# A streaming encoder layer on one core: token operands of the pairs in a pool of their own, two branch jobs run together, convolutions spread differently

## The chip, the cores and the metric

The kernel runs on one core of one Trainium2 chip. Its time is device microseconds (us) of one execution. Three executions of the kernel before took 2276.99, 2281.00 and 2281.24 us, median 2281.0. The profiled execution is another one, of 2278.88 us.

The core's engines run side by side, each in the order of its own queue: TensorE (PE, matmuls), VectorE (DVE), ScalarE (ACT), GpSimd (POOL) and SyncE (SP), which here issues all the DMAs.

## The reference

One inference step of a layer with 1024 channels, for 1024 prompt tokens and 32 sample tokens. All is float32:

```
x    = layer_norm(x)
proj = x @ w_in                                   # 1024 x 17424
y_a  = a * conv3(..) * silu(z_a)                  # branch 0
y_b  = RGLRU(conv4(x_b)) * silu(z_b)              # branch 1
y_c  = silu(LN(conv31(GLU(..)))) * silu(z_c)      # branch 2
y_d  = RMSNorm(gated_delta(silu(conv4(q,k,v)))) * silu(z_d)   # branch 3
mixed = sum over n of sigmoid(gate_n) * (y_n @ w_branch[n])
x    = layer_norm(ALPHA * x + mixed @ w_out)
```

The convolutions are causal and depthwise, with 3, 4, 31 and 4 taps. The new convolution and recurrence states are outputs too.

## The kernel before, in words

Activations lie channels by tokens: a tile is 128 channels x 1056 tokens (1024 + 32), 528 KB. A float32 product is made of three matmuls on rounded halves: the high part of the weights by the high and by the low part of the activations, and the low part of the weights by the high part (wh by xh, wh by xl, wl by xh). The code that splits a weight is `wsplit`: one DMA (L177), one ACT cast (wh, L179), one DVE subtraction (wl, L181).

The work goes in stages.

1. **Jobs.** A `Job` is one 128-channel output of an input projection: three chunks of 352 tokens, 24 matmuls each (L212), and per chunk an eviction by ACT or DVE. While they run, queues of generators are stepped between groups of eight matmuls (`bg`): the gated-delta work, the triangular elimination of branch D on DVE (`eliminate`, L546 and L547), short convolutions, and in `qc` the 31-tap convolutions of branch C (`c_conv`, one DVE step per tap, L297). The rate of a queue is the number of its steps per three calls of `bg`. The first four of the eight 31-tap convolutions (`N_CONV`) are made here; the input of the other four is written to DRAM (`d_cp`) for later.
2. **Pairs.** 36 `Pair`s compute two 128-channel outputs each by a seven-product scheme on quarters of the activations (L1046). Their token operands are built once (`build_t`): xh and xl themselves, and six tiles TH and TL for sums and differences (product operands t1, t2, t4). A product is 2 chunks of 12 matmuls. Each pair uses the three pairs of PSUM banks a, c and b once. Products 1, 3, 5 and 6 are added up in banks a: after products 1, 3 and 5, ACT copies the running sum away (`keep`, `mu`, L1058) before the next product adds to it, and after product 6 ACT evicts it (L1080). A queue `qm` steps in the pairs: the four late 31-tap convolutions, their statistics, then eight `b_mix` (branch B: convolution, gates with 18 matmuls L1153, a scan L1173).
3. **Branches**, in the order 0, 3, 2, 1. For each, eight staged tiles (`stage_y`: two loads `d_t` and `d_z`, one DVE multiply, L1274; branch 2 has more) are split into yh (ACT cast, L1247) and yl (DVE subtraction, L1248) by `put_y`, and eight branch jobs of 72 matmuls multiply them with `w_branch`, are scaled by a gate tile loaded from DRAM, and are added up in DRAM (`d_mix`). The first and the last job of a branch have their row tiles k as the outer loop over three banks (`all_chunks`, L224), the others take a chunk at a time (L212). The tiles for the next branch are staged while the jobs run.
4. **Output projection**, 9 token tiles (L1333), layer norm and store.

Memory is reused between stages: what the pairs use, xh, xl, TH and TL, lies on one stack (`xstack`), which is closed after the last pair; the tiles yh, yl and the sixteen staging tiles `st` are allocated in its place (`yp`). So the first load of branch 0 stands after the last product of the last pair. The instructions of an engine are put in their final order by a scheduler that also moves work forward; the order on each engine is therefore quoted from the built program where it matters.

Of the kernel before, what the change touches and what calls it, by code (L numbers as in the profile page):

```python
# [53 lines left out]
def encoder_step(ctx: ExitStack, tc: tile.TileContext, I, O):  # L54
# [173 lines left out]
    XR = (lambda k: xh[:, k, :], lambda k: xl[:, k, :])  # L228

# [589 lines left out]
    qc = queue("conv", 1.45)  # L819
    ORDER = "A0 A1 X0 C0 X1 A2 C1 X2 A3 C2 X3 A4 C3 X4 A5 C4 X5 C5 C6 C7"  # L820
    N_CONV = 4
# [122 lines left out]
    TH = {j: w2.tile([128, 4, HT], F32R, name=f"th{j}") for j in (1, 2, 4)}  # L944
    TL = {j: w2.tile([128, 4, HT], F32R, name=f"tl{j}") for j in (1, 2, 4)}
# [46 lines left out]
    class Pair:  # L992
# [10 lines left out]
        def prep(self):  # L1003
# [17 lines left out]
            split("21", a12, wpool, "wl")  # L1021
            yield
            dve.tensor_sub(a12, a12, s)
            dve.tensor_sub(a21, a11, a21)
            split("t3", a21, w2, "o3")
            yield
            split("t4", a22, w2, "o4")
            yield
            split("22", a12, w2, "o2")

        def run(self, step):
# [22 lines left out]
            def keep(name):  # L1054
                def then(c, b):
                    if c == 0:
                        mu[name] = w2.tile([128, HT], F32, name="mu", bufs=2)
                    act.copy(mu[name][:, c * HC:(c + 1) * HC], b)  # L1058
                return then
# [27 lines left out]
            product(4, "21", "b", True, plus(0, 0, "m1"), True)  # L1087
            product(5, "t3", "a", False, m7)
            product(6, "t4", "a", False, m4, True)
            product(7, "22", "c", False, plus(0, 1, "u1"), True)  # L1090

    def run_pairs(pairs, after):
# [4 lines left out]
        for n, p in enumerate(pairs):  # L1097
# [10 lines left out]
            def step(j):  # L1108
# [9 lines left out]
                elif j >= 6 and after is not None and nxt is None:  # L1118
                    after.load()
# [80 lines left out]
    qm = queue("mix", 0.52 * PARTS)  # L1200
# [37 lines left out]
    run_pairs(pairs, wb[branches[0]][0])  # L1238
# [11 lines left out]
    def st(dtype=F32, n=T):  # L1250
        return yp.tile([128, n], dtype, name="st", tag="st", bufs=16)

    staged = []

    def stage_y(n):

        if n == 2:
            mu, rs = st(), st()
            for i, t in enumerate((mu, rs)):
                src = d_mr[9 * i:9 * i + 1, 0:1]  # L1260
                sp.dma_start(t, bass.AP(tensor=src.tensor, offset=src.offset, ap=[[0, 128], [1, T]]))
        for k in range(8):
            t, z = st(), ev() if n == 2 else st()
            sp.dma_start(t, d_t[n][k])
            sp.dma_start(z, d_z[n][k])
            yield
            yield
            if n == 2:
                dve.tensor_sub(t, t, mu)
                yield  # L1270
                dve.tensor_mul(t, t, rs)
# [19 lines left out]
    for _ in stage_y(branches[0]):  # L1291
        pass
# [115 lines left out]
```

## Time and profile before

| | |
|---|---|
| median of three executions | 2281.0 us |
| the profiled execution | 2278.88 us, of which its span is 2277.2 us |
| PE busy | 2201.5 us (97% of the span) |
| DVE busy | 1645.7 us (72%) |
| ACT busy | 1004.1 us (44%) |
| 31-tap and short convolution steps on DVE, accc (L297) | 335.1 us |
| matmuls of the pairs by line (chain) | 28% of the chain of work that ended last |

How to read it: the span is the time from the first to the last instruction; 1.7 us of the execution lie around it. PE is nearly always busy, so what an edit changes is read from the stretches where PE waits or runs at its lower clock: the granted clock is given as a share of 2.4 GHz, and 0.50 is the lower level, 1.2 GHz. A DMA counts from its issue to its landing.

### The profile page before, as it was taken

To read this page: it belongs to the slowest core of one execution; us is meant where nothing else is said; L and a number is where in the kernel's file an instruction comes from. 1 tells how busy PE (TensorE), PEld (TensorE's weight loads), DVE (VectorE), ACT (ScalarE), POOL (GpSimd) and SP (SyncE) were. 2 spreads that over 40 slices of the span, in tenths; PEclk is the share of its full clock that TensorE was granted. 3 is DMA by queue.
4 is the path that set the end of the run, shared out by engine and by line. 5 is a ranking of instruction groups with operands and counts; after the bars stand their busy time and mean duration, and the time that the engine had idled before them with its cause. 6 is when DMAs were issued, how large, how long until landed. Compare 5 with 4: busy or idle time off the path is not lost.

```text
span 2277.2 us, 38625 instructions
## 1 busy us (share of the span) xinstructions
PE 2201.5 (97%) x15334; PEld 2143.5 (94%) x15334; DVE 1645.7 (72%) x2668; ACT 1004.1 (44%) x1938; POOL 168.2 (7%) x257
## 2 busy tenths in 40 slices
PE   7999989998999999999999999999999799999998
PEld 7999989998989999999999999999999799999976
DVE  8586665699998783779789796666666759835565
ACT  4587776311153443333444444566666335302200
POOL 3211011100000000100000000000000001000043
PEclk9999999999999999999999999999999899999999
DMA  6154443411265554223333333233344889965422
GB/s 231 44 144 127 122 129 106 137 54 29 59 214 164 180 159 120 77 77 109 128 111 111 106 128 113 96 124 117 115 135 141 318 305 321 330 212 170 134 94 75
DMA packets 197872, 322.56 MB, mean 142 GB/s; under 512 B 52762, under 2 KB 117100, under 8 KB 197372
## 3 DMA queue, kind: packets, MB, share of 16 engines
q1 hardware_dynamic: 197691, 320.10, 43.6%
q8 instruction: 120, 1.97, 0.4%
q14 instruction: 61, 0.49, 0.1%
HBM read 210.55 MB, written 109.49 MB: 141 GB/s over the span
## 4 chain that ended last, share of the span: by engine, by line
PE 65%; DVE 10%; ACT 2%; DMA 2%; issue 1%; SPq 0%; DVEq 0%; ACTq 0%
PE mm L1046 28%; PE mm L212 24%; PE mm L1333 4%; PE mm L224 3%; DVE accc L297 2%; DVE bt L546 2%; DVE bx L547 2%; PE aux L1153 1%; DMA wr<-in_w_in 1%; PE aux L668 1%; PE aux L661 1%; PE aux L681 1%; PE aux L652 1%; PE aux L680 1%; DVE yl L1248 1%
## 5 line engine op out<-in xcount | busy, mean ns | idle before, releaser
L297 DVE SCALAR_TENSOR_TENSOR accc<-padc,cols,accc 128x1086 f32<-128x1086 f32 (+2 forms) x250 | 335.1, 1340 | 14.2 <-ACT accc L294 12.7
L212 PE MATMUL mm<-xh,wh 128*128 128x352 f32 (+2 forms) x1600 | 301.4, 325 | 9.7 <-DVE padc L719 4.5
L212 PE MATMUL mm<-xh,wl 128*128 128x352 f32 (+2 forms) x1568 | 296.1, 328 | 6.0 <-DVE wl L181 6.0
L212 PE MATMUL mm<-xl,wh 128*128 128x352 f32 (+2 forms) x1600 | 299.4, 325 | 0.0
L212 PEld LDWEIGHTS mm<-xh,wh 128*128 128x128 f32 x1600 | 260.0, 190 | 11.7 <-issue 5.1
L212 PEld LDWEIGHTS mm<-xh,wl 128*128 128x128 f32 x1568 | 257.7, 192 | 9.4 <-DVE wl L181 7.1
L212 PEld LDWEIGHTS mm<-xl,wh 128*128 128x128 f32 x1600 | 259.2, 190 | 1.5 <-issue 0.2
L179 ACT CAST wh<-wr 128x1024 fp32r<-128x1024 f32 x96 | 100.8, 1050 | 286.1 <-PE mm L212 231.9
L1046 PE MATMUL mm<-xh,o 128*128 128x264 f32 x1152 | 221.5, 283 | 0.0
L1046 PEld LDWEIGHTS mm<-xh,o 128*128 128x128 f32 x1152 | 183.1, 188 | 0.0
L1046 PE MATMUL mm<-xl,o 128*128 128x264 f32 x576 | 163.3, 283 | 0.0
L181 DVE TENSOR_TENSOR wl<-wr,wh 128x1024 fp32r<-128x1024 f32 x96 | 116.8, 1217 | 42.9 <-ACT wh L179 23.6
L1058 ACT COPY mu<-mm 128x264 f32<-128x264 f32 x216 | 80.9, 377 | 113.8 <-PE mm L1046 110.9
L1064 DVE TENSOR_TENSOR ev<-mm,mu 128x264 f32<-128x264 f32 x216 | 91.3, 427 | 46.9 <-PE mm L1046 33.7
L1046 PE MATMUL mm<-th,o 128*128 128x264 f32 x576 | 112.1, 286 | 3.2 <-ACT mu L1058 3.0
L1227 DVE TENSOR_TENSOR ev<-mm,ev 128x352 f32<-128x352 f32 x90 | 46.2, 521 | 93.7 <-PE mm L212 88.0
L1046 PE MATMUL mm<-xh,wh 128*128 128x264 f32 x576 | 112.1, 285 | 0.9 <-DVE ev L807 0.9
L1046 PE MATMUL mm<-xh,wl 128*128 128x264 f32 x576 | 111.9, 285 | 0.0
L1046 PE MATMUL mm<-th,wh 128*128 128x264 f32 x576 | 111.6, 285 | 0.0
L1046 PE MATMUL mm<-th,wl 128*128 128x264 f32 x576 | 111.5, 284 | 0.0
L1046 PEld LDWEIGHTS mm<-xl,o 128*128 128x128 f32 x576 | 108.2, 188 | 0.0
L212 PE MATMUL mm<-yh,wh 128*128 128x352 f32 x576 | 105.9, 324 | 1.5 <-ACT yh L1247 1.5
(323 smaller groups left out, 4884.4 us busy)
## 6 DMA issues: line engine op xcount, KB each, us to landing
wr<-in_w_in SPq DMA_DIRECT2D x137, 512.0 KB, 3.9
d_z<-ev SPq DMA_DIRECT2D x64, 264.0 KB, 2.1
d_gate<-ev SPq DMA_DIRECT2D x64, 264.0 KB, 2.1
st<-d_t SPq DMA_DIRECT2D x32, 528.0 KB, 7.5
wr<-in_w_branch SPq DMA_DIRECT2D x32, 512.0 KB, 4.8
ev<-d_gate SPq DMA_DIRECT2D x30, 528.0 KB, 4.5
st<-d_z SPq DMA_DIRECT2D x24, 528.0 KB, 7.7
d_mix<-ev SPq DMA_DIRECT2D x24, 528.0 KB, 3.9
```

The lines of the kernel that those rows point to most:

```text
L179: act.copy(hi, raw)
L181: dve.tensor_sub(lo, raw, hi.bitcast(F32))
L212: pe.matmul(ps[:, :c[1]], lhsT=w[:, k, :], rhs=r(k)[:, cs(c)], start=(n == 0), stop=(n == len(todo) - 1))
L224: pe.matmul(ps[:, :c[1]], lhsT=w[:, k, :], rhs=r(k)[:, cs(c)], start=(n == 0), stop=(n == len(todo) - 1))
L297: dve.scalar_tensor_tensor(acc, pad[:, i:i + W], col(name, ci, i), acc, op0=OP.mult, op1=OP.add)
L546: dve.tensor_tensor(tv, a[:, j + 1:, j:j + 1].to_broadcast([P, n, m]), x[:, j:j + 1, 0:m].to_broadcast([P, n, m]), op=OP.mult)
L547: dve.tensor_tensor(x[:, j + 1:, 0:m], x[:, j + 1:, 0:m], tv, op=OP.subtract)
L1046: pe.matmul(b, lhsT=w[:, wo + k, :], rhs=XS[name](p, k)[:, sl], start=(start and n == 0), stop=(stop and n == 11), skip_group_check=True)
L1058: act.copy(mu[name][:, c * HC:(c + 1) * HC], b)
L1064: dve.tensor_add(res[i][:, a:a + HC], b, mu[name][:, c * HC:(c + 1) * HC])
L1227: dve.tensor_mul(G[d][:, cs(c)], ps, G[d][:, cs(c)])
L1333: pe.matmul(ps, lhsT=a[k][:, ts], rhs=w[k][:, hs], start=(n == 0), stop=(n == len(todo) - 1))
```

## The change

Four edits.

- **Convolutions.** The queue of the 31-tap convolutions in the job stage steps at 1.1 in place of 1.45, and three of them (`N_CONV`) in place of four are made there; five in place of four wait for the pairs, whose queue `qm` steps at 0.55 in place of 0.52 per `bg`.
- **Product order in a pair.** The product of "21" moves from place 4 to place 6; t3 and t4 move up to 4 and 5. The preparation of the operands is reordered alike, and `mu` has three buffers.
- **Token operands and staging.** TH and TL go into a pool `tt` on the right side of memory. In the last pair, product 5 is then the last that reads it; `ending(5)` closes it and puts the pool `stp` (12 staging tiles) there, issues the loads of the first five row tiles of branch 0, and after product 6 multiplies two of them. `ending` also stops `qm` in the last pair and loads the weights of the first two branch jobs. Four tiles `sl` take over what else used staging tiles.
- **`together`.** The first two jobs of branch 0 run row tile by row tile over six banks: 18 matmuls per row tile k. `qm` goes on after them.

```diff
+    def together(jobs, after):
+        for j in jobs:
+            j.load()
+            j.before()
+        pss = [[mmt() for _ in range(NCH)] for _ in jobs]
+        for k in range(KT):
+            for j, b in zip(jobs, pss):
+                for i, (w, r) in enumerate(j.products()):
+                    for ps, c in zip(b, chunks):
+                        pe.matmul(ps[:, :c[1]], lhsT=w[:, k, :], rhs=j.rhs[r](k)[:, cs(c)], start=(k == i == 0), stop=(k == KT - 1 and i == 2))
...
-    qc = queue("conv", 1.45)
+    qc = queue("conv", 1.1)
...
-    N_CONV = 4
+    N_CONV = 3
...
-    TH = {j: w2.tile([128, 4, HT], F32R, name=f"th{j}") for j in (1, 2, 4)}
+    ttc = ExitStack()
+    tt = ttc.enter_context(tc.tile_pool(name="tt", bufs=1, side="right"))
+    TH = {j: tt.tile([128, 4, HT], F32R, name=f"th{j}") for j in (1, 2, 4)}
...
-            product(4, "21", "b", True, plus(0, 0, "m1"), True)
-            product(5, "t3", "a", False, m7)
-            product(6, "t4", "a", False, m4, True)
+            product(4, "t3", "a", False, m7)
+            product(5, "t4", "a", False, m4, True)
+            product(6, "21", "b", True, plus(0, 0, "m1"), True)
...
-    qm = queue("mix", 0.52 * PARTS)
+    MIX = 0.55
+    qm = queue("mix", MIX * PARTS)
...
+    def ending(j):
+        if j == 1:
+            qm.rate = 0.0
+        if j in (2, 4):
+            wb[branches[0]][j // 2 - 1].load()
+        if j == 5:
+            ttc.close()
+            stp.append(ctx.enter_context(tc.tile_pool(name="stp", bufs=1, side="right")))
+            first_y.append(stage_y(branches[0], 5))
+            next(first_y[0])
+            next(first_y[0])
+        if j == 6:
+            while len(staged) < 2:
+                next(first_y[0])
...
-        run(wb[n][:7], wb[n][7])
+        if b == 0:
+            together(wb[n][:2], wb[n][2])
+            qm.rate = MIX
+            run(wb[n][2:7], wb[n][7])
+        else:
+            run(wb[n][:7], wb[n][7])
```

Three places of the built programs. Line numbers of the changed kernel are 18 to 53 higher; L564 and L565 there are L546 and L547 of before (the elimination), L315 is L297 (a convolution step), L811 is L793 (an eviction of branch A), L1295 is L1274 (the staging multiply), L1327 is L1248 (yl), L1084 is L1064 (an eviction of the pairs), L1209 is L1189 (a gate store), L1277 and L1278 are L1264 and L1265 (the staging loads).

DVE in the job stage, before, between the elimination steps of 855 and 799 elements:

```order
L546 TENSOR_TENSOR bt<-ba,bx 128x855
L297 SCALAR_TENSOR_TENSOR accc<-padc,cols,accc 128x1086
L547 TENSOR_TENSOR bx<-bx,bt 128x19x45
L297 SCALAR_TENSOR_TENSOR accc<-padc,cols,accc 128x1086
L546 TENSOR_TENSOR bt<-ba,bx 128x828
L297 SCALAR_TENSOR_TENSOR accc<-padc,cols,accc 128x1086
L547 TENSOR_TENSOR bx<-bx,bt 128x18x46
L297 SCALAR_TENSOR_TENSOR accc<-padc,cols,accc 128x1086
L546 TENSOR_TENSOR bt<-ba,bx 128x799
```

and the same stretch of the changed kernel:

```order
L564 TENSOR_TENSOR bt<-ba,bx 128x855
L811 TENSOR_TENSOR pad<-mm,ev 128x352
L565 TENSOR_TENSOR bx<-bx,bt 128x19x45
L315 SCALAR_TENSOR_TENSOR accc<-padc,cols,accc 128x1086
L564 TENSOR_TENSOR bt<-ba,bx 128x828
L315 SCALAR_TENSOR_TENSOR accc<-padc,cols,accc 128x1086
L565 TENSOR_TENSOR bx<-bx,bt 128x18x46
L811 TENSOR_TENSOR pad<-mm,ev 128x320
L564 TENSOR_TENSOR bt<-ba,bx 128x799
```

Two convolution steps stand in this stretch in place of four, and evictions that PE's banks wait for come between.

DVE at the start of branch 0, before: the staging multiplies and yl, with work of a `b_mix` (L1156 to L1166) between them:

```order
L1141 TENSOR_TENSOR gwl<-gwr,gwh 128x256
L1274 TENSOR_TENSOR st<-st 128x1056
L1156 TENSOR_TENSOR ev<-ev,accc 128x1056
L1248 TENSOR_TENSOR yl_19159<-st,yh_19158 128x1056
L1274 TENSOR_TENSOR st<-st 128x1056
L1248 TENSOR_TENSOR yl_19163<-st,yh_19162 128x1056
L1274 TENSOR_TENSOR st<-st 128x1056
L1162 SCALAR_TENSOR_TENSOR padc<-accc,padc 128x1056
L1248 TENSOR_TENSOR yl_19167<-st,yh_19166 128x1056
```

and in the changed kernel, where two steps of a `b_mix` (L315) stand ahead and the last eviction of the pairs:

```order
L315 SCALAR_TENSOR_TENSOR accc<-padc,cols,accc 128x1059
L1084 TENSOR_TENSOR ev<-mm,mu 128x264 x2
L315 SCALAR_TENSOR_TENSOR accc<-padc,cols,accc 128x1059
L1084 TENSOR_TENSOR ev<-mm,mu 128x264
L1295 TENSOR_TENSOR st<-st 128x1056
L1327 TENSOR_TENSOR yl_19088<-st,yh_19087 128x1056
L1295 TENSOR_TENSOR st<-st 128x1056
L1327 TENSOR_TENSOR yl_19092<-st,yh_19091 128x1056
L1295 TENSOR_TENSOR st<-st 128x1056
```

Multiply and subtraction alternate through all eight row tiles, and the `b_mix` work is gone from between them.

SP at the same place, before: the first loads (d_t_96, d_z_100) after the gate stores of the last pair's products,

```order
L177 DMA wr<-in_w_branch 128x1024
L1189 DMA d_gate<-ev 128x528
L1264 DMA st<-d_t_96 128x1056
L1189 DMA d_gate<-ev 128x528
L1265 DMA st<-d_z_100 128x1056
L1264 DMA st<-d_t_96 128x1056
L1265 DMA st<-d_z_100 128x1056
```

and in the changed kernel, where the two gate stores ahead of the first load belong to the last pair's products 4 and 5, and that of product 6 comes after ten loads:

```order
L177 DMA wr<-in_w_branch 128x1024
L1209 DMA d_gate<-ev 128x528
L1209 DMA d_gate<-ev 128x528
L1277 DMA st<-d_t_96 128x1056
L1278 DMA st<-d_z_100 128x1056
L1277 DMA st<-d_t_96 128x1056
L1278 DMA st<-d_z_100 128x1056
```

The loads have moved ahead of two products of the last pair.

## Rows read from the trace of the kernel before

**Rows 1.** The page, head and part 1: span; busy us, share, instructions.

```profile
span 2277.2 us, 38625 instructions
PE 2201.5 (97%) x15334; PEld 2143.5 (94%) x15334; DVE 1645.7 (72%) x2668; ACT 1004.1 (44%) x1938; POOL 168.2 (7%) x257
```

**Rows 2.** Windows by stage: engines' busy us (instructions), PEclk granted, DMA share, GB/s.

```profile
520.00:600.00 80.00, 68.76 (x389) 67.30 (x388) 80.00 (x87) 11.98 (x16) 2.58 (x5) 0.91 0.16 48
660.00:672.00 12.00, 7.53 (x37) 6.89 (x37) 12.00 (x26) 5.84 (x7) 0.00 (x0) 0.72 0.53 156
...
1400.00:1764.00 364.00, 360.61 (x2925) 359.01 (x2924) 233.28 (x374) 221.00 (x385) 9.23 (x32) 1.00 0.36 121
1765.90:1812.60 46.70, 33.90 (x163) 30.68 (x162) 35.54 (x35) 20.63 (x23) 4.25 (x2) 0.85 0.80 306
1812.60:2152.00 339.40, 339.40 (x2123) 339.40 (x2123) 214.87 (x279) 102.87 (x101) 8.80 (x10) 1.00 0.73 253
```

**Rows 3.** PE timeline, job stage: start, us, instruction [idle before <- releaser].

```profile
540.94 4.37 PE L212 MATMUL mm<-xh,wl 128*128 128x352 f32 x16 [3.78 <-DVE wl L181]
...
556.26 2.39 PE L212 MATMUL mm<-xh,wh 128*128 128x352 f32 x7 [4.49 <-DVE padc L719]
```

**Rows 4.** DVE timeline, job stage, from the 34th to the 41st weight split.

```profile
490.18 1.22 DVE L181 TENSOR_TENSOR wl<-wr,wh 128x1024 fp32r<-128x1024 f32 x1
...
552.10 1.35 DVE L297 SCALAR_TENSOR_TENSOR accc<-padc,cols,accc 128x1086 f32<-128x1086 f32 x1
553.36 1.18 DVE L546 TENSOR_TENSOR bt<-ba,bx 128x975 f32<-128x975 f32 x1
...
599.46 1.22 DVE L181 TENSOR_TENSOR wl<-wr,wh 128x1024 fp32r<-128x1024 f32 x1
```

**Rows 5.** PE timeline, the last pair's products 6 and 7 and the first branch jobs.

```profile
1759.80 0.28 PE L1046 MATMUL mm<-th,o 128*128 128x264 f32 x1
...
1762.73 0.28 PE L1046 MATMUL mm<-xh,o 128*128 128x264 f32 x1
...
1765.63 0.48 PE L1153 MATMUL aux<-ev,gwh 128*128 128x352 f32 x2
...
1794.36 1.38 PE L212 MATMUL mm<-yh,wh 128*128 128x352 f32 x4
1795.54 1.08 PE L224 MATMUL mm<-yl,wh 128*128 128x352 f32 x3
...
1811.30 1.45 PE L212 MATMUL mm<-yh,wl 128*128 128x352 f32 x8
1812.59 1.45 PE L212 MATMUL mm<-yh,wh 128*128 128x352 f32 x8
```

**Rows 6.** DVE and ACT timelines, one row tile's staging and the next multiply.

```profile
1778.87 1.25 DVE L1274 TENSOR_TENSOR st<-st 128x1056 f32<-128x1056 f32 x1
...
1780.15 1.07 ACT L1247 CAST yh<-st 128x1056 fp32r<-128x1056 f32 x1
...
1782.43 1.25 DVE L1274 TENSOR_TENSOR st<-st 128x1056 f32<-128x1056 f32 x1
```

**Rows 7.** SP timeline, and for the first and second load the time to landing.

```profile
1763.76 0.32 SPq L1189 DMA_DIRECT2D d_gate<-ev  x1
1766.29 0.32 SPq L1264 DMA_DIRECT2D st<-d_t  x1
...
1767.42 0.42 SPq L1265 DMA_DIRECT2D st<-d_z  x1
...
DMA to landing us min/median/max: 3.8/3.8/3.8
...
DMA to landing us min/median/max: 4.6/4.6/4.6
```

**Rows 8.** PE's waits in the pairs: total us, times, longest; and one of them.

```profile
PE mm L1046 <- ACT mu L1058: 3.0, 2, 1.9
...
1522.09 0.39 PE L1046 MATMUL mm<-th,o 128*128 128x264 f32 x1 [1.92 <-ACT mu L1058]
```

More of the change, by code (lines that the diff above doesn't have):

```diff
@@ L1117, in step @@
                     next(st["nxt"], None)
-                elif j >= 6 and after is not None and nxt is None:
-                    after.load()
+                elif nxt is None:
+                    after(j)
             p.run(step)
@@ L1237, in encoder_step, with st, sl, stage_y @@
     wb = {n: [wb_job(n, d, n != branches[0], n == branches[-1]) for d in range(8)] for n in branches}
-    run_pairs(pairs, wb[branches[0]][0])
+    stp, first_y = [], []
+    def st(dtype=F32, n=T):
+        return stp[0].tile([128, n], dtype, name="st", tag="st", bufs=12)
+    def sl(dtype=F32, n=T):
+        return yp.tile([128, n], dtype, name="sl", tag="sl", bufs=4)
+    staged = []
+    def stage_y(n, ahead=1):
+        tz = []
+        def load():
+            k = len(tz)
+            if k < 8:
+                tz.append((st(), st()))
+                sp.dma_start(tz[k][0], d_t[n][k])
+                sp.dma_start(tz[k][1], d_z[n][k])
+        if n == 2:
+            mu, rs = sl(), sl()
+            for i, t in enumerate((mu, rs)):
+                src = d_mr[9 * i:9 * i + 1, 0:1]
+                sp.dma_start(t, bass.AP(tensor=src.tensor, offset=src.offset, ap=[[0, 128], [1, T]]))
+        for _ in range(ahead):
+            load()
+        yield
+        yield
+        for k, (t, z) in enumerate(tz):
+            if n == 2:
+                dve.tensor_sub(t, t, mu)
+                yield
+                dve.tensor_mul(t, t, rs)
+                act.activation(t, t, AF.Silu, scale=col("c_g", k), bias=col("c_bb", k))
+                yield
+            dve.tensor_mul(t, t, z)
+            load()
+            staged.append(t)
+            yield
+            yield
+    def ending(j):
[12 more added lines that the diff above has]
+                next(first_y[0])
+    run_pairs(pairs, ending)
     xstack.close()
@@ L1248, in put_y @@
         dve.tensor_sub(Y_L[i], y, Y_H[i].bitcast(F32))
[L1250 to L1271, printed above, removed]
-                act.activation(t, t, AF.Silu, scale=col("c_g", k), bias=col("c_bb", k))
-                yield
-            dve.tensor_mul(t, t, z)
-            staged.append(t)
     woh, wol = [], []
@@ L1290, in encoder_step @@
     qn = queue("norm", 1.5)
-    for _ in stage_y(branches[0]):
-        pass
     for b, n in enumerate(branches):
         for k in range(8):
+            while not staged:
+                next(first_y[0])
             put_y(k, staged.pop(0))
```

23 lines of the change are left out of this document (15 added, 8 removed).

## The prediction

> **What bounds the kernel now.** I read the page first: PE is busy 2201.5 of 2277.2 us [rows 1]. A change can therefore pay only where PE stands idle or runs slow, so next came PE's busy time and granted clock by stage [rows 2], then the timelines around the stretches that fall out. The reader is to see three things there. First, from 520 to 600 PE is busy 68.76 of 80 us at a clock of 0.91 while DVE is busy all 80: 11.2 us idle, and 0.09 x 68.76 = 6.2 us lost to the clock, 17.4 together. PE waits there for DVE, for a weight split and for an eviction [rows 3]. A second such place is 660 to 672: 4.5 us idle and 0.28 x 7.53 = 2.1 by the clock, 6.6. Second, in the pairs PE is all but full (360.61 of 364 in the later part, where the 18 matmuls of each b_mix are among the work). Third, the two first branch jobs: the pairs' last matmul ends at 1765.9, the third branch job starts at 1812.59 [rows 5], 46.7 us for 144 matmuls. At the pace of 1811.30 to 1812.59, eight in 1.29 us, 144 take 144 x 0.161 = 23.2. PE was idle 12.8 us in this stretch, ran 18 b_mix matmuls, and had a clock of 0.85 [rows 2]. After it, up to 2152, PE is never idle.
>
> The sum is made against the profiled execution, 2278.88 us, which is its span and 1.7 us around it. The median of the three executions is 2281.0, 2.1 above, and I add that at the end.
>
> **The first branch jobs (tt, stp, ending, together).** Before, the first load is issued at 1766.29, after the last product [rows 7]. In the changed kernel it stands behind the gate store of product 5, two products from the end; by the old trace that is a product ending at 1759.80 in place of one ending at 1765.6. A gate store leaves SP 1.0 us after its product (product 6 of before ends at 1762.73, its store is issued at 1763.76 [rows 5, 7]). So the first load is issued at 1759.8 + 1.0 + 0.35 = 1761.2, the second 0.5 later. They landed after 3.8 and 4.6 us, so the first row tile is complete at 1766.3. The multiply (1.25) and the cast (1.07 [rows 6]) make yh ready at 1768.7; before, PE began on the first yh at 1777.7. The last DVE eviction of the pairs is done by then. Queued behind these loads on SP are the gate stores of products 6 and 7, which are read by branch 1, far later, and the gate tiles of the first two jobs, which are wanted only at their eviction.
>
> From there on the tiles come one per cycle of multiply, cast and subtraction: the order on DVE alternates strictly, so the next multiply waits for the subtraction, which waits for ACT's cast. In before one such cycle took 1782.43 - 1778.87 = 3.56 us [rows 6]. PE needs 18 x 0.161 = 2.9 us per tile, so the cycle is what ends last: the eighth yh is ready at 1768.7 + 7 x 3.56 = 1793.6. Six matmuls later PE waits for yl (1.3 us after yh), and twelve more end at 1793.6 + 1.3 + 1.9 = 1796.8. That is 15.8 us before 1812.6. But one b_mix's 18 matmuls, which ran in the gap for nothing, now run elsewhere beside full PE: 18 x 0.161 = 2.9 back. Net -12.9, of which the stopped queue, the early loads and the six banks all are part. Bounds: if the tiles came faster than PE, 1768.7 + 23.2 = 1791.9, that is -17.8; if PE ran all of it at its lower clock, the rows at 1794.36 and 1795.54 give four matmuls in 1.18 us, 0.295 each, 144 x 0.295 = 42.5, end 1811.2, and with the 2.9 it is +1.5. I stay at the cycle, since even a slow first tile (5.3 us) is made up by its slack of 0.66 per tile.
>
> The clock speaks against it here. In before it fell to 0.5 around 1794 [rows 5] while PE's work came in pieces of one tile, and the changed kernel still works tile by tile with a small wait in each. The Trainium skill (TensorE: Matmul & The Clock Gate, section "HAM oscillation — how this bites in real kernels") describes a kernel whose short bursts of matmuls each end in a wait for an operand, and each start again at the lower clock; by that rule the bound of +1.5 would be the forecast for this stretch. The trace agrees for that one spell; over the stretch its clock is 0.85, with gaps larger than those I expect.
>
> **The convolutions in the job stage.** From the 34th to the 41st weight split DVE was never idle, 490.18 to 599.46, 109.3 us [rows 4]. In the built programs this stretch holds 26 steps of the 31-tap convolution, 57 of the elimination and 23 small instructions before, 23, 48 and 17 after. A convolution step is 1.26 us from start to start (552.10 to 553.36), an elimination step 1.18 at 553.36 and falling, about 0.9 for those that leave, the small ones some 0.3: 3 x 1.26 + 9 x 0.9 + 6 x 0.3 = 13.7 less. Three splits further, at the 44th, the difference is 36 against 32 convolution steps and 79 against 72 of the by then short elimination steps, by the same prices about 9.7. As DVE sets the pace here, PE cannot win more than DVE sheds: -9 of the 17.4. Bounds 0 (the waits only move) and -17.4. The loss at 660 to 672 stands where 18 convolution steps followed each other on DVE; in the new order that burst is gone, but 11 convolution steps and some 70 small ones stand close together three jobs later. I take -2, between -6.6 and +5.5 (the new burst needs about 5.5 us more of DVE than the old one by the same prices).
>
> **The pairs.** The seven products are the same. What is new is a second tight hand-off: t3 now follows t2 directly on banks a, so ACT's copy must be done within the other chunk, as it already had to be between t3 and t4. That old one made PE wait 3.0 us in all 36 pairs, 1.92 the longest [rows 8]. A second one of its kind costs the same 3. DVE gets a fifth convolution and 6% more steps per bg; DVE was busy 233 of 364 us in the later pairs [rows 2], so this lies beside PE, at nothing; if the cover fails it shows as waits for evictions, in the upper bound. Bounds: 0, and +10 if every pair waits a seventh of that longest (36 x 0.27). The mu buffers and the operand order cost nothing: each buffer is free a product before it is written.
>
> **The branches after.** About two more b_mix fall behind the pairs than before. DVE was busy 214.87 of 339.4 us there with PE at 339.40 [rows 2], so they are covered, except where their DVE work meets the staging of branch 2: +1, between 0 and +6.
>
> **Sum.** -12.9 - 9 - 2 + 3 + 1 = -19.9: 2278.9 - 19.9 = 2259.0 for the profiled kind of execution, 2261 beside the median of 2281.0.
>
> **Rivals.**
> - *The job stage gives nothing*: DVE is still its bound and the waits move to the new burst. For it: after the edit DVE still needs nearly 96 us where PE's seven jobs of 11.6 need 81. Against it: the lead PE had before its first wait. Time 2261 + 11 = 2272. Chance 0.14.
> - *The clock takes the first branch jobs*: all 144 matmuls at 0.295, by the clock rows above; 2261 + 12.9 + 1.5 = 2275. Against it: the clock came back to 1.00 by 1804 with the same kind of work. Chance 0.10.
> - *The loads don't come early* (the change doesn't do what it says): SP is held by an earlier wait, or the transfers queue behind the weights, and the first tile is staged as far behind the last product as before, 9 us later than I say: 2270. For it: SP issues in order and three weight loads stand just ahead. Chance 0.08.
> - *Slower: the second hand-off*. ACT has activation-table loads and b_mix's long activations ahead of the copy in many pairs; if t3 waits as 1522.09 did, 1.92 us in each of 36 pairs, it is 69 us. It decides from 0.55 us per pair (19.9 / 36). At 1.1 us mean, 2261 - 3 + 40 = 2298. Against it: the same hand-off between t3 and t4 reached 0.55 twice in 36. Chance 0.06.
> - *Better*: all 17.4 of the job stage and the tiles faster than PE: 2261 - 8.4 - 4.9 = 2248. Chance 0.08.
>
> **How the numbers follow.** The forecast has the chance that is left, 0.54; its own range is 2252 to 2270. About 0.2%, 4.6 us, is what a measurement of this kernel can tell from no change, so faster means below 2276.4. The forecast, the better case, the lost job stage and the late loads all end there for the most part (0.54 + 0.08 + 0.11 + 0.07), and a good third of the clock case: 0.84. I take 0.82 for faster, 0.10 for the same, 0.08 for slower, the hand-off case and some of what I don't see. The range 2247 to 2276 leaves out the hand-off case and the tails.
>
> **What would show it.** Right: the first staging load some 4 us before the pairs' last matmul, yh from 2.8 us behind it, multiplies 3.56 us apart, the third branch job about 31 us behind the pairs; fewer than 8 us of PE idle and clock loss from 520 to 600; waits of PE for mu twice as many as before. Wrong: a first yh later than 6 us, a granted clock near 0.5 through the two jobs, or PE's idle time in the job stage moved to behind 640.

## The result, and the profile after

The changed kernel takes 2257.65 us (median of four runs, 2254.03 to 2260.95) against 2280.91 us for the kernel before (2276.99 to 2281.24): ratio 0.9902, 95% interval 0.9881 to 0.9922. The prediction said 2261, between 2247 and 2276, and faster with a chance of 0.82. The profiled execution took 2259.44 us, where the prediction's sum, made for an execution of that kind, said 2259.0; its span is 2257.7 us, before it was 2277.2 [rows 1].

The page, head and part 1 of the changed kernel (busy us, share of the span, instructions), answering to [rows 1]:

```profile
span 2257.7 us, 38700 instructions
PE 2198.2 (97%) x15334; PEld 2139.7 (95%) x15334; DVE 1645.8 (73%) x2668; ACT 1006.8 (45%) x1939; POOL 162.0 (7%) x257
```

The work is the same. What has changed is where PE stands still. The windows by stage, laid where the changed kernel does what [rows 2] show (columns as there); the fourth is from the last pair matmul to the third branch job, the fifth is as long as its counterpart of before:

```profile
520.00:600.00 80.00, 76.43 (x469) 76.07 (x468) 80.00 (x83) 10.44 (x14) 3.52 (x6) 0.98 0.14 42
660.00:672.00 12.00, 10.34 (x72) 9.71 (x73) 10.58 (x30) 5.18 (x15) 0.00 (x0) 0.86 0.54 155
1400.00:1747.00 347.00, 346.87 (x2825) 346.00 (x2824) 248.10 (x386) 203.97 (x358) 7.93 (x26) 1.00 0.37 121
1748.00:1782.20 34.20, 27.88 (x146) 24.66 (x145) 22.10 (x21) 10.95 (x12) 0.00 (x0) 0.90 0.88 351
1782.20:2121.60 339.40, 336.94 (x2092) 335.92 (x2091) 241.29 (x303) 128.52 (x131) 12.47 (x20) 0.99 0.77 266
```

Between 520 and 600 PE is idle 3.6 us in place of 11.2, at a clock of 0.98 in place of 0.91, while DVE is still busy all 80 us. In the pairs PE is full. The start of branch 0 takes 34.2 us in place of 46.7. But in the branches PE now stands still for 2.5 us of 339.4, where before it was never idle.

In the job stage both waits of [rows 3] are gone; the first that is left between 500 and 700 comes 57 us later than the first of before, with a smaller one behind it (PE timeline of the changed kernel; two more, of 1.79 and 2.19 us, come at 661 and 675):

```profile
598.29 2.13 PE L212 MATMUL mm<-xh,wl 128*128 128x352 f32 x6 [3.57 <-DVE wl L181]
604.22 1.07 PE L212 MATMUL mm<-xh,wh 128*128 128x352 f32 x5 [0.86 <-DVE padc L737]
```

What DVE does in that stretch became shorter. Its 34th and 41st weight split in the changed kernel, answering to [rows 4]:

```profile
487.20 1.22 DVE L181 TENSOR_TENSOR wl<-wr,wh 128x1024 fp32r<-128x1024 f32 x1
...
583.75 1.22 DVE L181 TENSOR_TENSOR wl<-wr,wh 128x1024 fp32r<-128x1024 f32 x1
```

From the one to the other it takes 96.6 us in place of 109.3, with 23 convolution steps and 48 elimination steps between them where the trace of before has 26 and 57. DVE is busy all the time in both, and PE now is too, at a clock of 1.00.

At the end of the pairs, SP's timeline in the changed kernel, and the time to landing of the second load, the first `d_z` (the trace has none for the first `d_t`), answering to [rows 7]:

```profile
1743.02 0.80 SPq L1209 DMA_DIRECT2D d_gate<-ev  x2
1743.92 0.42 SPq L1277 DMA_DIRECT2D st<-d_t  x1
1744.38 1.05 SPq L1278 DMA_DIRECT2D st<-d_z  x1
...
DMA to landing us min/median/max: 6.9/6.9/6.9
```

and PE's timeline, answering to [rows 5]:

```profile
1747.90 0.28 PE L1066 MATMUL mm<-xh,o 128*128 128x264 f32 x1
...
1753.90 1.54 PE L240 MATMUL mm<-yh,wh 128*128 128x352 f32 x4 [5.72 <-ACT yh L1326]
...
1782.22 1.45 PE L212 MATMUL mm<-yh,wh 128*128 128x352 f32 x8
```

The first load goes out 4.0 us before the last pair matmul, as forecast. But the second, which completes the first row tile, lands after 6.9 us, not 4.6, and PE begins on the first yh 5.7 us behind the end of the last pair matmul (6.0 behind its start), not 2.8. From there the tiles come at the forecast pace. DVE and ACT, the staging cycle that answers to [rows 6]:

```profile
1751.41 1.26 DVE L1295 TENSOR_TENSOR st<-st 128x1056 f32<-128x1056 f32 x1 [1.88 <-DMA st<-d_z]
...
1752.78 1.07 ACT L1326 CAST yh<-st 128x1056 fp32r<-128x1056 f32 x1 [2.48 <-DVE st L1295]
...
1758.62 1.25 DVE L1295 TENSOR_TENSOR st<-st 128x1056 f32<-128x1056 f32 x1
1761.02 1.26 DVE L1327 TENSOR_TENSOR yl<-st,yh 128x1056 fp32r<-128x1056 f32 x1 [1.14 <-ACT yh L1326]
1762.19 1.25 DVE L1295 TENSOR_TENSOR st<-st 128x1056 f32<-128x1056 f32 x1
```

1762.19 - 1758.62 = 3.57 us, in which DVE waits 1.14 us for ACT and ACT some 2.5 us for DVE. PE's clock in three parts of this start (windows):

```profile
1748.00:1754.00 6.00, 0.28 (x3) 0.10 (x1) 2.90 (x4) 2.19 (x3) 0.00 (x0) 0.74 1.02 412
1754.00:1758.00 4.00, 4.00 (x14) 3.79 (x15) 2.86 (x3) 1.07 (x1) 0.00 (x0) 0.53 1.02 414
1758.00:1782.00 24.00, 23.41 (x131) 20.57 (x130) 16.14 (x15) 7.49 (x8) 0.00 (x0) 1.00 0.83 328
```

It fell while PE stood idle, was near its lower level of 1.2 GHz for the first tile, and was at 2.4 GHz for all the rest. The last wait that is new stands in branch 0, for the seventh `b_mix`, which ran in the branches before too, but without a wait:

```profile
1921.31 0.72 PE L1173 MATMUL aux<-ev,gwh 128*128 128x352 f32 x2 [2.28 <-ACT ev L1164]
```

### The profile page after: what moved, and what is told of

It is laid out like the page before. It is cut to its first block, busy times and chain, and to the rows that moved or that the text cites. A ratio compares the mean times of both kernels' runs of the same rounds, so it can differ in the third digit from the quotient of the medians.

```text
span 2257.7 us, 38700 instructions
## 1 busy us (share of the span) xinstructions
PE 2198.2 (97%) x15334; PEld 2139.7 (95%) x15334; DVE 1645.8 (73%) x2668; ACT 1006.8 (45%) x1939; POOL 162.0 (7%) x257
## 4 chain that ended last, share of the span: by engine, by line
PE 70%; DVE 9%; DMA 3%; issue 2%; ACT 1%; SPq 0%; DVEq 0%; ACTq 0%
PE mm L1066 31%; PE mm L212 26%; PE mm L1391 4%; PE mm L224 2%; DVE accc L315 2%; DVE bt L564 1%; PE aux L1173 1%; DVE bx L565 1%; DMA Gb<-d_gc 1%; PE aux L679 1%; PE aux L686 1%; DVE yl L1327 1%; PE aux L699 1%; PE aux L698 1%; PE aux L670 1%
## 5 line engine op out<-in xcount | busy, mean ns | idle before, releaser
L315 DVE SCALAR_TENSOR_TENSOR accc<-padc,cols,accc 128x1086 f32<-128x1086 f32 (+2 forms) x250 | 335.1, 1341 | 10.8 <-ACT accc L312 9.4
L1084 DVE TENSOR_TENSOR ev<-mm,mu 128x264 f32<-128x264 f32 x216 | 91.2, 426 | 30.9 <-ACT mu L1078 16.0
L1030 ACT CAST o<-wr 128x512 fp32r<-128x512 f32 x108 | 66.8, 619 | 102.4 <-PE mm L1066 86.5
L212 PE MATMUL mm<-yh,wh 128*128 128x352 f32 x552 | 100.8, 324 | 0.0
```

The source lines that it names most:

```text
L212: pe.matmul(ps[:, :c[1]], lhsT=w[:, k, :], rhs=r(k)[:, cs(c)], start=(n == 0), stop=(n == len(todo) - 1))
L315: dve.scalar_tensor_tensor(acc, pad[:, i:i + W], col(name, ci, i), acc, op0=OP.mult, op1=OP.add)
L1030: act.copy(t[:, 0:4], src)
L1084: dve.tensor_add(res[i][:, a:a + HC], b, mu[name][:, c * HC:(c + 1) * HC])
```

## The experiments

Each kernel was timed against the kernel before on the same chip, and the ratios are to those runs. The stages are read from one profiled execution of each, in us: the first pair matmul (end of the job stage); from there to the start of the last pair matmul; from there to the third branch job; from there to the end of the last branch matmul; the sum of these three; and how many of the eight `b_mix` run in each of them.

```
                              jobs   pairs  start  rest   sum     b_mix  ratio (95%)
before                       1006.1  759.4  47.1  351.6  1158.1  5/1/2
changed                       994.1  753.8  34.3  362.4  1150.5  4/0/4  0.9902 (0.9881-0.9922)
e1  conv numbers alone        996.1  753.3  44.4  360.0  1157.7  4/0/4  0.9935 (0.9915-0.9956)
e2  conv numbers undone      1006.8  759.1  33.8  355.1  1148.0  5/0/3  0.9943 (0.9927-0.9960)
e4  conv rate alone          1000.7  761.0  48.7  351.6  1161.3  5/1/2  0.9962 (0.9945-0.9980)
e3  number of convs alone    1004.1  755.2  43.6  359.7  1158.5  4/0/4  0.9992 (0.9981-1.0003)
e11 product order alone      1005.6  759.0  44.4  351.8  1155.2  5/1/2  0.9988 (0.9978-0.9997)
e5  jobs one by one           996.0  753.3  40.3  364.3  1157.9  4/0/4  0.9936 (0.9920-0.9951)
e7  late loads                993.6  752.9  35.5  360.5  1148.9  4/0/4  0.9897 (0.9880-0.9914)
e8  GpSimd multiplies         996.3  753.6  35.5  359.5  1148.6  4/0/4  0.9900 (0.9885-0.9914)
e9  pairs' queue at 0.65      996.9  765.4  32.8  348.8  1147.0  7/0/1  0.9889 (0.9872-0.9906)
e12 staging in halves         991.2  754.1  30.2  363.4  1147.7  4/0/4  0.9885 (0.9863-0.9908)
e10 two convs, 0.85, 0.65     991.0  760.9  32.0  356.5  1149.4  5/0/3  0.9886 (0.9864-0.9907)
e13 e10 and e12 together      991.9  760.8  30.7  356.4  1147.9  5/0/3  0.9887 (0.9871-0.9904)
```

The changed kernel, e1, e5, e7, e8, e9 and e12 have the same two numbers for the convolutions of the job stage (1.1 and three), and their job stages end between 991.2 and 996.9: about 3 us either way is what one profile can tell there.

**Theory and rival.** My theory: the gain has two independent halves, the job stage (convolutions) and the start of branch 0, and what the pairs and branches show is one thing seen twice, `b_mix` moved from the one to the other. Rivals: one half is all of it; or inside the second half, the early loads and not the two jobs together make the gain.

### e1 and e2: each half alone

```diff
 # e1, in the kernel before
-    qc = queue("conv", 1.45)
-    N_CONV = 4
+    qc = queue("conv", 1.1)
+    N_CONV = 3
-    qm = queue("mix", 0.52 * PARTS)
+    qm = queue("mix", 0.55 * PARTS)
 # e2, in the changed kernel: the same three, the other way round
```

> The kernel before with the three numbers of the convolutions alone (1.1, three convolutions, 0.55). My theory: the job stage gives its 12 us whatever comes later, so the first pair matmul is at about 994 in place of 1006; some 4 of the 12 are given back behind the pairs, where more b_mix run, since the end of the pairs is as before: 2270, between 2267 and 2273. Rival: the job stage's gain belongs to DVE work that PE meets again in the pairs and branches, all of it given back: 2279 to 2281. Second rival: nothing is given back, 2269 or less.

> The changed kernel with the three numbers of the convolutions as before (1.45, four convolutions, 0.52). My theory: the first pair matmul is back at about 1006 (+12), the start of branch 0 keeps its 34 us from the last pair matmul to the third branch job, and the branches give some 4 us back, since less b_mix stands behind the pairs: 2265, between 2262 and 2268. Rival, all the time came from the end of the pairs: 2258, as the changed kernel. Rival, all from the convolutions: 2279 or more.

Measured: e1 2267.78 us (2261.47 to 2268.53), e2 2268.03 (2266.51 to 2270.08), before 2280.47 beside them. Each half gives about half, in its own place: e1 ends the job stage at 996.1 and has nearly the start of before (44.4 against 47.1), e2 ends it at 1006.8 and has the start of the changed kernel (33.8). Neither is all. The ratios multiply to 0.9878, which is 5 us less than the 0.9902 of the whole change and just outside its interval (0.9881 to 0.9922); the intervals of e1 and e2 leave room for that, so whether the halves add in full stays open. e2 lies just outside what I expected (2262 to 2268). What I expected wrongly is that e1 would give some of it back: its rest is 8.4 us longer, but its pairs are 6.1 and its start 2.7 shorter, so that behind the job stage the sum is 1157.7 against 1158.1.

### e4 and e3: the rate or the number of the convolutions

```diff
 # e4, in the kernel before
-    qc = queue("conv", 1.45)
+    qc = queue("conv", 1.1)
 # e3, in the kernel before
-    N_CONV = 4
+    N_CONV = 3
-    qm = queue("mix", 0.52 * PARTS)
+    qm = queue("mix", 0.55 * PARTS)
```

> The kernel before with the queue of the 31-tap convolutions at 1.1 in place of 1.45, still four of them in the job stage. My theory (DVE sheds work between 490 and 600, which is what PE waits for): the waits between 537 and 590 go, some 10 us, but the fourth convolution then ends later and is made in the tail of the stage: first pair matmul between 996 and 1001, time 2271 to 2276. Rival (it is the number of convolutions that counts): the first pair matmul stays at 1004 to 1007, 2279 to 2282.

> The kernel before with three in place of four convolutions in the job stage (and 0.55), their rate kept at 1.45. My theory: the waits between 537 and 590 stay, since the rate sets the work of VectorE there, and only the later loss goes: first pair matmul at 1001 to 1004, 2274 to 2278 with what the branches lose. Rival, the number of convolutions is what counts, and the job stage ends at 996 as it does with both edits: 2268.

Measured: e4 2273.03 us against 2280.47, e3 2276.09 against 2276.72. PE's timeline in the job stage of e3, its waits between 500 and 600:

```profile
541.07 5.06 PE L212 MATMUL mm<-xh,wl 128*128 128x352 f32 x16 [3.79 <-DVE wl L181]
556.38 2.32 PE L212 MATMUL mm<-xh,wh 128*128 128x352 f32 x7 [3.69 <-DVE padc L719]
587.34 0.95 PE L212 MATMUL mm<-xh,wl 128*128 128x352 f32 x2 [3.21 <-DVE wl L181]
```

and in e4 the first one after 500:

```profile
600.77 5.06 PE L212 MATMUL mm<-xh,wl 128*128 128x352 f32 x16 [3.58 <-DVE wl L181]
```

With the number alone the waits of [rows 3] stand where they stood. With the rate alone they are gone until 600, as in the changed kernel, since what DVE has between two weight splits has changed: between the 34th and the 41st, e4's trace has the 23 convolution steps and 48 elimination steps of the changed kernel, in 96.6 us, and e3's the 26 and 57 of before, in 109.3. But the fourth convolution is then made later: DVE is busy 213.07 of the 300 us from 700 to 1000 in e4, 201.97 in the kernel before, 177.25 in the changed one. The stage ends at 1000.7, and all kernels with both numbers changed end it before 997. What of PE's time that costs stays open.

### e11: the order of the products alone

```diff
-            product(4, "21", "b", True, plus(0, 0, "m1"), True)
-            product(5, "t3", "a", False, m7)
-            product(6, "t4", "a", False, m4, True)
+            product(4, "t3", "a", False, m7)
+            product(5, "t4", "a", False, m4, True)
+            product(6, "21", "b", True, plus(0, 0, "m1"), True)
```

(with the preparation in the same order and three `mu` buffers, in the kernel before)

> The kernel before with the new order of the products in a pair alone (t3 and t4 before 21, with the preparation of their operands and the third mu buffer). The prediction's step: a second tight hand-off costs PE 3 us more of waits for mu, the pairs take 762 us, 2284. What the changed kernel's trace suggests: the waits for mu go, the pairs take 3 us less, 756 us, 2278. Rival, the order does nothing and the pairs of the changed kernel were shorter only because one b_mix fewer ran in them: 759, 2281.

Measured: 2278.28 us against 2280.47, and the pairs take 759.0 us against 759.4. PE's waits in the pairs of e11 (total us, times, longest):

```profile
PE mm L1046 <- ACT mu L1058: 3.1, 4, 1.2
```

and one of them on PE's timeline, at the new hand-off (t3, whose operand is xh):

```profile
1689.43 0.39 PE L1046 MATMUL mm<-xh,wl 128*128 128x264 f32 x1 [1.17 <-ACT mu L1058]
```

The waits have doubled in number, as the prediction said, but their sum is 3.1 us where [rows 8] have 3.0: the new hand-off makes PE wait twice, 1.7 us, and at the old one (t4) the waits fell from 3.0 to 1.4. In sum the second hand-off costs nothing that can be measured. The rival with no effect fits the pairs; the 2 us by which the time is shorter lie in the start (44.4 against 47.1), and no run explains them.

### e5 and e7: two jobs together, or early loads

```diff
 # e5, in the changed kernel
-        if b == 0:
-            together(wb[n][:2], wb[n][2])
-            qm.rate = MIX
-            run(wb[n][2:7], wb[n][7])
-        else:
-            run(wb[n][:7], wb[n][7])
+        if b == 0:
+            qm.rate = MIX
+        run(wb[n][:7], wb[n][7])
 # e7, in the changed kernel: from ending() to behind the last pair
     run_pairs(pairs, ending)
     xstack.close()
+    ttc.close()
+    stp.append(...)
+    first_y.append(stage_y(branches[0], 5))
```

> The changed kernel with the first two jobs of branch 0 one after the other, the first by row tiles and the second by chunks, as in the kernel before; the early loads stay. My theory: PE has only nine matmuls for each row tile of the first job (1.45 us against a cycle of 3.57), waits 2.1 us in each, and starts the second job when the eighth tile is there: the third job starts 8 x 1.45 = 11.6 us behind the last tile, against 2.9 + the rest now, so some 8 us later than in the changed kernel; time 2264 to 2267. Rival, the early loads alone make the gain and together does nothing: 2258. Rival, the shorter bursts of PE let its clock fall to 0.5 as in the kernel before: 12 us later or more, 2270.

> The changed kernel with the pool of the token operands closed, the staging pool opened and the first loads issued only after the last product of the last pair; the two jobs still run together. My theory: the load is issued some 1.5 to 2 us behind the last pair matmul in place of 4.3 ahead, lands in 4 us as in the kernel before, so the first yh comes 4 to 5 us later and everything behind it too: 2262. Rival, the transfers were slowed by their early start (they took 6.9 us in place of 3.8), so that lateness costs little: 2259 or less. Rival, the early load is the whole gain at this place: 2270.

Measured: e5 2268.47 us, e7 2258.94, before 2281.6 beside both. With early loads and the jobs one by one, the sum behind the job stage is 1157.9, that of the kernel before. With late loads and the jobs together it is 1148.9, and the time is not to be told from the changed kernel's (0.9897 and 0.9902). The ratios say the same: e5 is e1 with the early loads, 0.9936 against 0.9935, and e7 is e1 with `together`, 0.9897. (All of them but e1 have the new order of products, which e11 priced.) So `together` makes the second half of the gain, and the early loads add nothing measurable to the time or to the sum. The start alone does get shorter by them (44.4 in e1 to 40.3 in e5, 35.5 in e7 to 34.3), but the rest is longer by as much or more (4.3 and 1.9); in e5, 2.5 of the 4.3 are waits for `b_mix`. Whether better placed `b_mix` would keep that gain was not tried.

For e7 I had expected 2262; the rival "the transfers were slowed by their early start, so that lateness costs little", with 2259 or less, came nearer. The edit moved less than its name says: SP still issued the first `d_t` 2.9 us before the last pair matmul (1746.52) and then held the first `d_z`, behind two gate stores, until 2.8 us after it. SP's timeline, and the time to landing of the second of the two loads:

```profile
1743.63 0.65 SPq L1277 DMA_DIRECT2D st<-d_t  x1
1747.04 2.23 SPq L1209 DMA_DIRECT2D d_gate<-ev  x2
1749.32 0.43 SPq L1278 DMA_DIRECT2D st<-d_z  x1
...
DMA to landing us min/median/max: 3.9/3.9/3.9
```

Against the last pair matmul this `d_z` goes out 6.3 us later than in the changed kernel, and it lands 3.0 us faster (3.9 in place of 6.9). DVE and PE show what becomes of the 3.2 us that are left:

```profile
1753.21 1.26 DVE L1295 TENSOR_TENSOR st<-st 128x1056 f32<-128x1056 f32 x1 [5.06 <-DMA st<-d_z]
...
1755.70 1.54 PE L240 MATMUL mm<-yh,wh 128*128 128x352 f32 x4 [8.90 <-ACT yh L1324]
...
1767.57 2.42 DVE L1295 TENSOR_TENSOR st<-st 128x1056 f32<-128x1056 f32 x2
1769.96 2.42 DVE L1325 TENSOR_TENSOR yl<-st,yh 128x1056 fp32r<-128x1056 f32 x2
1772.31 1.25 DVE L1295 TENSOR_TENSOR st<-st 128x1056 f32<-128x1056 f32 x1
```

The first yh is 9.2 us behind the last pair matmul, 3.2 later than in the changed kernel. But in this program two multiplies follow each other, and two subtractions, so that ACT's casts run beside DVE: two tiles in 1772.31 - 1767.57 = 4.74 us in place of 2 x 3.57, and the third job comes 35.5 us behind, 1.2 later. So what e7 shows is that loads issued later cost little here: half of the lateness is won back by faster landing, and most of the rest by that order on DVE. What was not tried is e7 with the strict order. As to the clock rival of e5: PE waits about 1.0 us in most of the tiles there, and the granted clock is 1.00 from 1762 on all the same.

### e8 and e12: the cycle of 3.57 us

```diff
 # e8, in the changed kernel
-            dve.tensor_mul(t, t, z)
+            if n == branches[0] and k % 2:
+                pool.tensor_tensor(t, t, z, op=OP.mult)
+            else:
+                dve.tensor_mul(t, t, z)
 # e12, in the changed kernel, branch 0 only
-            dve.tensor_mul(t, t, z)
+            for h in HALVES:
+                dve.tensor_mul(t[:, h], t[:, h], z[:, h])
...
-        act.copy(Y_H[i], y)
-        dve.tensor_sub(Y_L[i], y, Y_H[i].bitcast(F32))
+        for h in HALVES:
+            act.copy(Y_H[i][:, h], y[:, h])
+        for h in HALVES:
+            dve.tensor_sub(Y_L[i][:, h], y[:, h], Y_H[i][:, h].bitcast(F32))
```

> The changed kernel with the staging multiply of every second row tile of branch 0 on GpSimd in place of VectorE. My theory: the cycle of multiply, cast and subtraction (3.57 us per row tile) is what PE waits for, and with every second multiply out of it the tiles come faster than PE needs (2.9 us): the third branch job starts 4 to 5 us earlier behind the last pair matmul (29 to 30 us in place of 34.0); 2254. Rival, the loads set the pace (they land at 3.6 us per tile at best): 0, 2258. Rival, GpSimd's multiply is so slow, or takes so much of VectorE's memory port, that it is late itself: 2260 or more.

> The changed kernel with the staging of branch 0 in halves: multiply, cast and subtraction each work on 528 of the 1056 tokens, so that ACT casts the first half while VectorE multiplies the second. My theory: the cycle falls from 3.57 us per row tile to 2.7 or 2.8, below the 2.9 that PE needs; PE then sets the pace unless the transfers do, which at 410 GB/s bring the 16 staging tiles and what else is in the queue in some 31 us from the first issue: the third branch job starts 29 to 31 us behind the last pair matmul in place of 32.9, 2255. Rival, the transfers set the pace from the fourth tile on, as they did with GpSimd's multiply: 33 us or more, 2258. The prediction's own cycle step held this part to be the one that ends last.

Measured: e8 2258.95 us against 2281.6, no gain; its third job is 35.5 us behind. The theory of e8 fell. Its GpSimd, DVE and ACT, the second multiply on GpSimd and the one beside it on DVE:

```profile
1760.38 2.80 POOL L1296 TENSOR_TENSOR st<-st 128x1056 f32<-128x1056 f32 x1 [1.92 <-DMA st<-d_z]
...
1760.77 3.52 DVE L1298 TENSOR_TENSOR st<-st 128x1056 f32<-128x1056 f32 x1
...
1764.32 2.04 ACT L1329 CAST yh<-st 128x1056 fp32r<-128x1056 f32 x2 [4.76 <-DVE st L1298]
...
1768.57 2.77 POOL L1296 TENSOR_TENSOR st<-st 128x1056 f32<-128x1056 f32 x1 [5.40 <-DMA st<-d_z]
```

The DVE multiply that takes 1.25 us elsewhere took 3.52 beside the one on GpSimd; it ended 1.1 us after that one (1760.38 + 2.80 = 1763.18), as if it had begun only then. The Trainium skill (SBUF — State Buffer, section "SBUF: two separate sides") says that the two engines share a pair of ports, that one instruction holds it to its end, and that a VectorE operation with two inputs in SBUF is blocked meanwhile; the trace agrees with that. And GpSimd's third multiply waited 5.40 us for its load. So the loads and the shared ports, the two rivals of e8, both show in the trace; no run parts them.

e12 does the same without GpSimd: 2251.85 us against 2276.72 beside it. DVE's timeline, three multiplies in a row and the longest wait:

```profile
1748.27 1.33 DVE L1297 TENSOR_TENSOR st<-st 128x528 f32<-128x528 f32 x2 [1.33 <-DMA st<-d_z]
...
1751.08 1.33 DVE L1297 TENSOR_TENSOR st<-st 128x528 f32<-128x528 f32 x2
...
1753.74 1.32 DVE L1297 TENSOR_TENSOR st<-st 128x528 f32<-128x528 f32 x2
...
1764.36 1.33 DVE L1297 TENSOR_TENSOR st<-st 128x528 f32<-128x528 f32 x2 [1.81 <-DMA st<-d_z]
```

and the window of the start (columns as in [rows 2]):

```profile
1745.60:1775.40 29.80, 25.57 (x144) 25.29 (x145) 23.82 (x38) 12.07 (x20) 0.00 (x0) 0.89 0.96 384
```

and the one wait of PE in it (total us, times, longest):

```profile
PE mm L240 <- ACT yh L1329: 4.3, 1, 4.3
```

The cycle is now 1753.74 - 1751.08 = 2.66 us, the third job 30.2 us behind the last pair matmul, as expected. So the cycle was what ended last in the changed kernel. What ends last now is the first tile and then PE itself: after the 4.3 us of waiting for the first yh it is busy without a pause, 25.6 us for the 144 matmuls that take 23.2 at the higher clock. The transfers are not far behind: the DMA engines are busy 0.96 of the start, at 384 GB/s, and DVE waits for loads, but none of these waits reaches PE. In the time of the whole kernel the step can't be told from the changed kernel (0.9863 to 0.9908 against 0.9881 to 0.9922).

### e9, e10 and e13: more in the pairs, fewer convolutions, and all together

```diff
 # e9, in the changed kernel
-    MIX = 0.55
+    MIX = 0.65
 # e10: that, and
-    qc = queue("conv", 1.1)
-    N_CONV = 3
+    qc = queue("conv", 0.85)
+    N_CONV = 2
 # e13: e10 with the halves of e12
```

> The changed kernel with the queue of the pairs stepped at 0.65 in place of 0.55 per bg, so that seven in place of four of the eight b_mix are done in the pairs. My theory: the 11 us that the branches lost are mostly b_mix matmuls that were moved, whose 2.9 us each are paid in the pairs just as well, so 9 us move back to the pairs without a gain; what goes are the waits near 1921 and some clock, 3 us: 2255. Rival, b_mix is cheaper in the pairs (VectorE is free there): 2250. Rival, the pairs' evictions on VectorE then come late: 2260 or more.

> The changed kernel with two in place of three 31-tap convolutions in the job stage (rate 0.85) and 0.65 for the queue of the pairs, which then has a sixth convolution. My theory: VectorE sheds some 40 us more in the job stage, of whose 8.4 us of idle PE between 500 and 700 and some 5 us of clock there a half goes; the first pair matmul at 988, 2252. Rival, what PE still waits for in the job stage is not the convolutions (the waits after 598 are for evictions and the last splits): 994 as before it, 2258. Rival, the sixth convolution brings VectorE late in the pairs: 2262 or more.

> The staging in halves and the two convolutions in the job stage together (0.85, two, 0.65, halves), in the changed kernel. My theory: the two act at different places, the halves at the start of branch 0 (5 us) and the convolutions in the job stage, so that they add: ratio to the kernel before 0.9870, between 0.985 and 0.989. Rival, one gives back what the other gains (as the three numbers and the staging gave back 2 of 25): 0.9885, no better than either.

Measured: e9 2258.12 us against 2281.6, e10 2252.64 against 2276.72, e13 2253.53 against 2279.55. e9 has three more `b_mix` in the pairs, which are 11.6 us longer, and three fewer behind them, where 13.6 us went: 3.9 us each in the pairs, 4.5 each in the rest, and a sum only 3.5 us shorter. Of that, 3.0 us each are busy PE in the pairs and 3.7 in the rest (762.6 against 753.6, 359.9 against 348.8); the rest is waits. So where a `b_mix` stands changes little, and the time (0.9889) can't be told from the changed kernel's; I had expected 3 us less. In e10 the waits between 500 and 602 are gone, and one came in their place:

```profile
602.83 2.71 PE L212 MATMUL mm<-xh,wh 128*128 128x352 f32 x8 [6.93 <-DVE padc L737]
```

The idle time of PE between 500 and 700 is 8.4 us with two convolutions as with three, so here the rival that it isn't the convolutions any more was right. e10 and e12 don't add (the rival of e13): in e10's program the multiplies were already partly two by two, and its start was 32.0 us without halves, 30.7 with them. The three best, e10, e12 and e13, have ratios of 0.9885 to 0.9887, and the changed kernel's 0.9902 lies in all their intervals: none is shown to beat it.

## Why the prediction was right

The time was 3.4 us from the forecast (2257.65 and 2261), and both places that were to carry it did. That the profiled executions agree to 0.4 us (2259.44 and 2259.0) is in part luck: the job stage gave 1.0 more than forecast, and what follows it 1.3 less, after larger errors there that cancel. By its steps:

- **Job stage**, -9 and -2: measured -12.0 (1006.1 to 994.1), -11.3 in the mean of all profiles with four and with three convolutions at these rates (1006.2, three profiles; 994.9, seven). The reason given (DVE sets the pace, and PE wins what DVE sheds) is borne out by e4 and e3, and the size by the trace: DVE sheds 12.7 us between the 34th and the 41st split where the prediction said 13.7. From 520 to 600 PE lost 5.1 us to idleness and clock in place of 17.4, below the 8 that were named as the sign, and from 660 to 672 3.1 in place of 6.6. Some 4 us of these 15.8 came back elsewhere in the stage: PE now idles 1.0 us from 600 to 660 and 2.8 from 672 to 990, where before it idled 0 and 0.2. The rival "gives nothing" fell, though DVE needs the "nearly 96 us" that spoke for it.
- **Start of branch 0**, 46.7 to 30.9, of which 2.9 is paid elsewhere: measured 46.8 to 34.0 from the end of the last pair matmul (47.1 to 34.3 from its start, as in the table). Here the step that mis-sized is the landing of the first tile, "they landed after 3.8 and 4.6 us": the second load took 6.9, with a weight load and two gate stores issued in the 2 us ahead, and the DMA engines at 412 GB/s from 1748 on. Before the first load of the old kernel SP had issued nothing for 2.5 us [rows 7], and in e7, with one gate store in the 2 us ahead, the same load took 3.9; no run varies this alone. The first yh was 2.9 us later than forecast, all but at the 6 us that were named as a sign of being wrong. The cycle of 3.56 us was right to 0.01 (3.57), and so was that it ends last, by e12.
- **What in that step makes the gain.** The prediction put the stopped queue, the early loads and the six banks into one sum. The runs part it: the two jobs together are worth 7 to 10 us (e5 against the changed kernel, by time and by sums of stages), the early loads nothing that can be measured. Stopping the queue in the last pair wasn't tried, since the built program is the same without it.
- **The clock** in the two jobs: the rival of 2275 fell. PE worked in pieces of one row tile with waits of a few tenths of a us between, and kept 2.4 GHz from 1758 on; the lower level came only in the 5.7 us in which it stood idle and in the first 4 us of matmuls behind them. Pieces of one tile with a wait in each were not enough to bring it; e5, with waits of 1.0 us, says the same.
- **Pairs**, +3: measured -5.6. The term for the second hand-off is 0 (e11). Of the 5.6, 2.4 are busy PE (756.0 to 753.6), for a `b_mix` that runs elsewhere, and 3.2 are idleness, nearly all of it the waits for mu (3.0 us), which are gone in the changed kernel; the sign "waits of PE for mu twice as many" failed. They come back with five or seven `b_mix` in the pairs (3.0, 2.7 and 2.6 us of PE's waits for mu in e2, e10 and e9), and are 0 in e1 and 1.2 in e3, which have four and the old order. So they go with that work more than with the order.
- **Branches**, +1 beside the 2.9: measured +10.8. The step "18 x 0.161 = 2.9" for a `b_mix` fits the pairs (3.0 in e9) but was too small here: two more of them cost 8.5 us of busy PE, and 2.5 us of waits came with them. Why the same 18 matmuls cost more here was not tried.

The last two errors have opposite signs and are in part the same error: of the two `b_mix` that moved to the branches, the prediction priced the one that had run in the gap; the matmuls of the one that had run in the pairs were counted in neither place. In the sum behind the job stage they cancel: forecast -8.9, measured -7.6, and -9.6 when the means of several profiles are taken (the changed kernel, e2, e7, e8 and e9: 1148.6; before, e1, e3, e4 and e11: 1158.2).

## What to carry to other kernels

Where two engines hand each tile to and fro, the pace is the sum of their steps, whatever the busy shares say: give the consumer more work per tile (two jobs on six banks), or cut the tile in halves so that the steps overlap; issuing the first load earlier moves only the first tile, and less than the time by which it is issued earlier if other transfers are just ahead of it. Work in a background queue is paid wherever it runs (here 3.9 us in one stage and 4.5 in the other), so compare stages only in sums over all places to which it can move. And a rate that spreads filler between the instructions that the bound engine waits for can be worth more than taking a quarter of the filler away.

## What the runs showed of the hardware

Two multiplies of the same shape on DVE and GpSimd did not run side by side: 3.52 us in place of 1.25 on DVE, and 2.80 on GpSimd. A load of 528 KB that landed in 3.8 us when SP had issued nothing for 2.5 us, and in 3.9 us with one gate store in the 2.2 us ahead (e7), took 6.9 us with a weight load, two gate stores and another load issued in the 2.2 us ahead of it. And the clock of PE stayed at its higher level through 24 us of bursts of 18 matmuls with a short wait in each (and in e5 with waits of 1.0 us), after it had fallen in 5.7 us of idleness.
